# Four tokens' one-hot rows in one broadcast comparison, and gathered rows paced later, in a PEER layer kernel

## The chip, the cores and the metric

The kernel runs on one core of a Trainium2 chip. The metric is the device time of one execution in microseconds, the median of three runs. Engines are named as in the profile: PE is TensorE's matmul, PEld its weight load, DVE is VectorE, ACT is ScalarE, POOL is GpSimd, SP is SyncE. An instruction that only issues a DMA is listed under the engine's queue (SPq, ACTq) or, on POOL, under POOL itself.

## What is computed

One decoder layer on 512 tokens of width 2048: normalisation, two groups of attention heads, an output projection, and then a product-key layer (PEER) whose part of the reference is this, cut to what matters:

```
s_half, i_half = top_k(scores of 2 halves, 16)          # per token and head, 8 heads
top_s, pos = top_k(sums of the two halves' scores, 16)
idx = i * 128 + j                                       # one of 16384 experts
g = softmax(top_s)
u = expert_u[ic];  a = einsum('cd,ced->ce', xc, u)
w = g * gelu(a)
y = einsum('ce,ced->cd', w, expert_v[ic])
```

Each token uses 8 x 16 = 128 experts, and each expert is a row of 2048 floats in `expert_u` and one in `expert_v`.

## The kernel before

About the first 1000 us hold attention, projections and the routing (the top-16 searches). The rest treats the tokens in two ways.

**Tokens 128 to 511, densely.** The "U half" multiplies all 16384 rows of `expert_u` with the 384 tokens, in 128 blocks of 128 rows (`u_block`, loop at L1020). A block is two half-blocks. For each, `u_turn` runs three half-blocks ahead: it issues the block's load in four DMAs (`u_load`, L858, two on SP's queue and two on ACT's), transposes 128x1024 on DVE (L870, `uT`), and `split` makes a high part on ACT (L117) and a low part on DVE (L118). Then come 24 matmuls into `pa` (L883 to L885). At the block's end ACT takes the gelu (L890) and POOL stores `acts_d` (L891). The "V half" (loop from L1050) multiplies the gated activations with the rows of `expert_v`: 16 groups x 4 column quarters x 4 pairs of weights are 256 calls of 18 matmuls (L191 to L193); each weight pair is again split on ACT and DVE, POOL makes the gated `wg` (L1041) ahead of time, and DVE adds the results into `hd` (L1060).

**The gates of these tokens** are spread out during the U half by `dense_gates`. For each of 384 tokens, `expand` makes a one-hot matrix of j on POOL (`oj`, L907), a bf16 one-hot matrix of i on DVE (`on`, L909, four buffers), and from that two gate-weighted versions on ACT (`oi`, L912, two instructions). Seven tokens later `merge` multiplies them on PE (`gps`, L921); ACT and DVE copy and add the result into `stage` (L930, L931), and after each 16 tokens ACT issues the store `gates_d` (L933), 24 stores in all.

**Tokens 0 to 127, by gathering.** `gathered` walks through 256 rows per token: 128 of `expert_u`, then 128 of `expert_v`. For each step POOL issues an indirect DMA (L966) that brings one row for each of 128 tokens (128 x 2048 floats, 1.05 MB) into one of three buffers `gt`, and DVE uses it, L974 in the u part and L977 in the v part. The last step stores `h[0]` (L982).

**What sets the order.** Each engine runs its instructions in an order that the framework fixes when the program is built, by the order in which they are written, by priorities and by a model of when operands are ready. Side work is fed by a `Filler`: each call of `run(budget)` adds to a credit (at most 4.0), and steps are written out while the credit is over zero, each step costing what it yields. A token of `dense_gates` costs 0.17, and each half-block gives it `share` = 36 / (124 - e), with e the first block of the loop. A gathered row costs 2.3; a half-block of the U half gives 1.2, a call of the V half 1.3. `gatherer.drain()` after the last call writes out what is left. The gatherer is `paced`: its instructions are held behind the latest marked DVE instruction.

Of the kernel before, what the change touches and what calls it, by code (L numbers as in the profile page):

```python
# [10 lines left out]
F32 = mybir.dt.float32  # L11
F32R = mybir.dt.float32r
BF16 = mybir.dt.bfloat16
# [3 lines left out]
ALU = mybir.AluOpType  # L17
# [15 lines left out]
PH, NK, TOPK = 8, 128, 16  # L33
SLOTS = PH * TOPK
TG = 128
TD = S - TG
# [16 lines left out]
def block_kernel(ctx, tc, x, positions, norm1_gain, w_in, q_a_gain, w_q_b, kv_a_gain, w_kv_b, mla_q_gain,  # L53
                 mla_k_gain, swa_q_gain, swa_k_gain, swa_sinks, rel_bias_table, group_out_gain, w_out,
                 norm2_gain, peer_w_q, peer_sub_keys, peer_u, peer_v, out):
    nc = tc.nc
# [10 lines left out]
    def pool(name, bufs=1, side=None, stack=ctx, **kw):  # L67
        return stack.enter_context(tc.tile_pool(name=name, bufs=bufs, side=side, reuse_waits="tile", **kw))
# [7 lines left out]
    def acc_tile(name="acc"):  # L76
        return psum.tile([128, 512], F32, name=name, tag="acc", bufs=5)

    def tp_tile(name="tp"):
        return psum.tile([128, 512], F32, name=name, tag="tp", bufs=3)  # L80
# [35 lines left out]
    def split(hi, lo, src):  # L116
        first[0] = nc.scalar.activation(hi, src, AF.Copy)  # L117
        mark[0] = nc.vector.tensor_tensor(lo, src, hi.bitcast(F32), op=ALU.subtract)  # L118
# [551 lines left out]
    for t in range(NT):  # L670
        for i, o in enumerate((o_mla, o_swa)):
# [4 lines left out]
                                           op0=ALU.mult, op1=ALU.mult)  # L676
# [67 lines left out]
    iotb = consts.tile([128, 128], BF16, name="iotb")  # L744
# [59 lines left out]
    def weigh(t, dst):  # L804
        e = exs[t]
        nc.scalar.activation(e, e, AF.Exp)
        z = small.tile([128, PH], F32, name="gz")
        nc.vector.tensor_reduce(z, e, axis=AX.X, op=ALU.add)
        rz = small.tile([128, PH], F32, name="grz")
        nc.vector.reciprocal(rz, z)  # L810
        nc.vector.tensor_tensor(dst.rearrange("p (h s) -> p h s", h=PH), e,
                                rz[:, :, None].to_broadcast([128, PH, TOPK]), op=ALU.mult)
# [49 lines left out]
    def u_turn(n):  # L862
        if n >= 2 * NK:
            return
        e, hf = divmod(n, 2)
        if hf == 0:
            u_load(e + 2)
        hi, lo = part_pair(n, [128, 8, 128])
        uT = up.tile([128, 8, 128], F32, name="uT")
        nc.vector.transpose(uT.rearrange("p k (b j) -> p b k j", j=32),  # L870
                            u_raw[e].rearrange("p b (k i) -> p b k i", k=KC)[:, :, hf * 8:hf * 8 + 8, :])
        split(hi, lo, uT)
        u_parts[n] = hi, lo

    def u_block(e, budget, pace=0.0):
        pa = acc_tile("pa")
        for hf in range(2):
            n = 2 * e + hf
            u_turn(n + 3)
            hi, lo = u_parts.pop(n)  # L880
            for k in range(8):
                kk = hf * 8 + k
                nc.tensor.matmul(pa[:, :TD], hi[:, k, :], xTd[0][:, kk, :], start=kk == 0, stop=False)  # L883
                nc.tensor.matmul(pa[:, :TD], hi[:, k, :], xTd[1][:, kk, :], start=False, stop=False)  # L884
                nc.tensor.matmul(pa[:, :TD], lo[:, k, :], xTd[0][:, kk, :], start=False, stop=kk == KC - 1)  # L885
            filler.run(budget)
            gatherer.run(pace)
        ga = xtp.tile([128, TD], F32, name="ga", bufs=2)
        with tc.issue_after(first[0].ins):
            nc.scalar.activation(ga, pa[:, :TD], AF.Gelu_apprx_tanh)  # L890
        nc.gpsimd.dma_start(acts_d[e], ga)  # L891
# [5 lines left out]
        yield 0.6  # L897

    def dense_gates():
        slT = [gb.tile([128, TD], F32, name=f"slT{r}") for r in range(2)]  # L900
        gT = [gb.tile([128, TD], F32R, name=f"gT{r}") for r in range(2)]
        hot, banks, stages = {}, {}, {}
        LAG = 7

        def expand(t):
            oj = gb.tile([128, NK], F32R, name="oj", bufs=LAG + 2)
            nc.gpsimd.tensor_scalar(oj, iot, slT[1][:, t:t + 1], None, op0=ALU.is_equal)  # L907
            on = gb.tile([128, NK], BF16, name="on", bufs=4)
            nc.vector.tensor_scalar(on, iotb, slT[0][:, t:t + 1], None, op0=ALU.is_equal)  # L909
            oi = gb.tile([128, 2, NK], F32R, name="oi", bufs=LAG + 2)  # L910
            for r in range(2):
                nc.scalar.activation(oi[:, r, :], on, AF.Copy, scale=gT[r][:, t:t + 1].bitcast(F32))  # L912
            hot[t] = oj, oi

        def merge(t):
            oj, oi = hot.pop(t)
            i = t % 2
            if i == 0:
                banks[t // 2] = acc_tile("gps")
            gps = banks[t // 2]  # L920
            nc.tensor.matmul(gps[:, i * 256:(i + 1) * 256], oj, oi.rearrange("p r i -> p (r i)"), start=True, stop=True)  # L921
            if i < 1:
                return
            g0, tb = t // GT, t % GT - 1
            if tb == 0:
                stages[g0] = gb.tile([128, NSG, GT, SG], F32, name="stage", bufs=2)
            stage = stages[g0]
            sums = gps.rearrange("p (t r g e) -> p r t g e", t=2, r=2, e=SG)
            dst = stage[:, :, tb:tb + 2, :].rearrange("p g t e -> p t g e")
            nc.scalar.activation(dst, sums[:, 0], AF.Copy)  # L930
            nc.vector.tensor_tensor(dst, dst, sums[:, 1], op=ALU.add)  # L931
            if tb == GT - 2:
                nc.scalar.dma_start(  # L933
                    bass.AP(tensor=gates_d.tensor, offset=gates_d.offset + g0 * GT * SG,
                            ap=[[TD * SG, 128], [128 * TD * SG, NSG], [1, GT * SG]]),
                    stage.rearrange("p g t e -> p g (t e)"))

        for t in range(1, NT):
            ts = slice((t - 1) * 128, t * 128)
            gt = gb.tile([128, SLOTS], F32, name="gt")  # L940
            weigh(t, gt)
            tp = tp_tile()
            for r in range(2):
                nc.tensor.transpose(tp[:, r * 128:(r + 1) * 128], ijs[t][:, r].rearrange("p h s -> p (h s)"), ident)
            nc.tensor.transpose(tp[:, 256:384], gt, ident)
            for r in range(2):
                nc.scalar.activation(slT[r][:, ts], tp[:, r * 128:(r + 1) * 128], AF.Copy)
            split(gT[0][:, ts], gT[1][:, ts], tp[:, 256:384])
            yield 0.6
        for t in range(TD + LAG):  # L950
            if t < TD:
                expand(t)
            if t >= LAG:
                merge(t - LAG)
            yield 0.17
# [28 lines left out]
    gatherer = Filler(paced=True)  # L984
# [5 lines left out]
    e = 0  # L990
# [11 lines left out]
    gb = pool("gb", stack=stg)  # L1002
    filler.add(dense_gates())
    share = 36.0 / (NK - 4 - e)
    gts, wgs, wb = {}, {}, {}

    def gate_tile(g):
        if g < NSG:
            gg = wp.tile([128, TD, SG], F32, name="gg", bufs=2)
            nc.sync.dma_start(gg, gates_d[g].rearrange("j (t e) -> j t e", e=SG))  # L1010
            gts[g] = gg

    def act_tile(e):
        if e < NK:
            wgs[e] = wp.tile([128, TD], F32, name="wg", bufs=AHEAD)
            nc.sync.dma_start(wgs[e], acts_d[e])
# [1 line left out]
    AHEAD = 5  # L1018
    wp = None
    while e < NK:  # L1020
        u_block(e, share, 1.2)
        e += 1
        if not filler.queue and wp is None:
            stg.close()
            wp = pool("wp", side="right")
            gate_tile(0)
            for i in range(AHEAD):
                act_tile(i)
# [22 lines left out]
    for g in range(NSG):  # L1051
        for c in range(4):
            acc = [acc_tile(), acc_tile(), tp_tile()]
            for i, w in enumerate(weights(v_rows[g * SG * 128:(g + 1) * SG * 128], SG, c * 512, 512, turn=4 * g + c)):
                k0 = 2 * i
                for t in range(NT - 1):
                    products(acc[t], lambda hl, kk, t: wb[g * SG + kk][hl][:, t * 128:(t + 1) * 128], t, k0, SG, w, 512)
                    if k0 == SG - 2:
                        hc = h[t + 1][:, c * 512:(c + 1) * 512]
                        mark[0] = nc.vector.tensor_tensor(hc, acc[t], hc, op=ALU.add)  # L1060
                        if g == NSG - 1:
                            nc.sync.dma_start(out[(t + 1) * 128:(t + 2) * 128, c * 512:(c + 1) * 512], hc)
                nxt = (g + 1) * SG
                if c < 3 and k0 < 4:
                    w_block(nxt + 2 * c + k0 // 2)
                if c == 3 and k0 > 2:
                    w_block(nxt + 4 + k0 // 2)
                gatherer.run(1.3)
    gatherer.drain()


# [23 lines left out]
```

## Time and profile before

| | us |
|---|---|
| median of three runs | 3193.74 |
| runs | 3190.99 to 3194.65 |
| profiled execution, its own time | 3190.16 |
| its span, first to last instruction | 3188.4 |

| engine | busy us | share of the span |
|---|---|---|
| PE | 3074.1 | 96% |
| DVE | 2431.3 | 76% |
| ACT | 1273.9 | 40% |
| POOL | 1275.9 | 40% |

Shares are means over stages with different limits, so the useful views are those by stretch of time: the busy time and the number of instructions of each engine, TensorE's granted clock, and the busy share of the 16 DMA engines. A pipelined matmul counts as busy for longer than it holds the engine, so PE's pace is better read from the count of matmuls in a stretch than from its busy time. The views of waits give for each pair of waiting and releasing instruction the total idle time, the number of waits and the longest; "issue" means that the engine waited for nothing the profile shows.

### The profile page before, as it was taken

What the parts mean: (1) busy time and instruction counts of PE and PEld (TensorE: products, weight loads), DVE (VectorE), ACT (ScalarE), POOL (GpSimd) and SP (SyncE); (2) the same over time, 40 slices, a digit from 0 to 9 for tenths busy, and PEclk for the clock granted to TensorE, in tenths of its full rate; (3) what the DMA queues carried; (4) which work ended last, traced back from release to release, by engine and by line L of the source; (5) the groups of instructions that cost most, each with busy time, mean ns of one, the idle gap of its engine ahead of it and who ended that gap; (6) DMA issues with size and microseconds to landing.
All of it is one profiled execution on the core that took longest, in us unless ns stands there. A gap on an engine that the chain in (4) does not pass through costs nothing.

```text
span 3188.4 us, 42942 instructions
## 1 busy us (share of the span) xinstructions
PE 3074.1 (96%) x15418; PEld 2688.7 (84%) x15418; DVE 2431.3 (76%) x3694; ACT 1273.9 (40%) x2438; POOL 1275.9 (40%) x1260
## 2 busy tenths in 40 slices
PE   8999999989988999899999999999999999999999
PEld 6977768868778999899999998977888888888887
DVE  5425654246999798889989897878888878878874
ACT  5434453232234465555655553332332223322231
POOL 0115320001223476577656654344434433534330
PEclk9998999999989999999999999999999999999999
DMA  5422222243336799999999999989888887878874
GB/s 171 121 80 77 67 96 93 93 129 83 75 94 176 200 285 274 277 268 301 290 286 294 268 281 294 312 320 346 310 318 308 323 312 299 317 286 311 324 265 159
DMA packets 307064, 731.68 MB, mean 229 GB/s; under 512 B 24098, under 2 KB 106274, under 8 KB 269730
## 3 DMA queue, kind: packets, MB, share of 16 engines
q1 hardware_dynamic: 175394, 343.01, 34.3%
q0 software_dynamic: 45056, 293.63, 25.2%
q10 hardware_dynamic: 86400, 92.29, 10.6%
q8 instruction: 122, 2.00, 0.3%
q14 instruction: 92, 0.75, 0.1%
HBM read 666.97 MB, written 61.87 MB: 229 GB/s over the span
## 4 chain that ended last, share of the span: by engine, by line
PE 54%; DVE 15%; DMA 3%; issue 3%; ACT 1%; ACTq 1%; POOL 1%; DVEq 0%; SPq 0%; POOLq 0%
PE acc L191 8%; PE acc L193 7%; PE acc L192 7%; PE pa L885 7%; PE pa L883 7%; PE pa L884 7%; PE tp L191 4%; PE tp L193 3%; PE tp L192 3%; DVE uT L870 3%; DVE wlo L118 3%; DVE gt L974 2%; DMA wg<-acts_d 1%; DVE ulo L118 1%; ACTq L858 1%
## 5 line engine op out<-in xcount | busy, mean ns | idle before, releaser
L885 PE MATMUL pa<-xTd,wlo 128*128 128x384 f32 x1536 | 523.9, 342 | 14.5 <-DVE wlo L118 14.4
L883 PE MATMUL pa<-xTd,whi 128*128 128x384 f32 x1536 | 524.8, 342 | 6.0 <-ACT ga L890 3.5
L884 PE MATMUL pa<-xTd,whi 128*128 128x384 f32 x1536 | 523.6, 341 | 0.0
L907 POOL TENSOR_SCALAR oj<-iot,slT 128x128 fp32r<-128x128 f32 x384 | 416.3, 1092 | 258.2 <-PE gps L921 256.7
L118 DVE TENSOR_TENSOR wlo<-wraw,whi 128x1024 fp32r<-128x1024 f32 (+3 forms) x229 | 285.7, 1254 | 299.3 <-ACT whi L117 292.7
L117 ACT ACTIVATE whi<-wraw 128x1024 fp32r<-128x1024 f32 (+3 forms) x229 | 233.3, 1023 | 515.2 <-PE acc L193 251.1
L966 POOL DMA_INDIRECT gt<-in_peer_v_dram,eidx x128 | 198.7, 1552 | 360.8 <-DVE h L977 329.1
L977 DVE SCALAR_TENSOR_TENSOR h<-gt,w,h 128x2048 f32<-128x2048 f32 x128 | 321.8, 2514 | 13.6 <-DMA gt<-in_peer_v_dram,eidx 13.6
L1041 POOL TENSOR_TENSOR wg<-wg,gg 128x384 f32<-128x384 f32 x128 | 224.1, 1771 | 222.7 <-DMA wg<-acts_d 201.2
L191 PE MATMUL acc<-whi,wh 128*128 128x512 f32 x768 | 307.8, 401 | 2.7 <-ACT wh L117 1.9
L885 PEld LDWEIGHTS pa<-xTd,wlo 128*128 128x128 f32 x1536 | 294.3, 192 | 17.5 <-DVE wlo L118 17.5
L912 ACT ACTIVATE oi<-on,gT 128x128 fp32r<-128x128 bf16 x768 | 253.0, 391 | 138.5 <-issue 76.7
L192 PE MATMUL acc<-wlo,wh 128*128 128x512 f32 x768 | 303.2, 395 | 5.0 <-DVE wlo L118 5.0
L193 PE MATMUL acc<-whi,wl 128*128 128x512 f32 x768 | 304.6, 397 | 0.5 <-DVE wl L118 0.5
L974 DVE CUSTOM_DVE_ANT_0 gt<-gt,xn 128x2048 f32<-128x2048 f32 x128 | 298.7, 2334 | 4.9 <-DMA gt<-in_peer_u_dram,eidx 4.9
L883 PEld LDWEIGHTS pa<-xTd,whi 128*128 128x128 f32 x1536 | 294.7, 192 | 8.0 <-ACT ga L890 3.8
L884 PEld LDWEIGHTS pa<-xTd,whi 128*128 128x128 f32 x1536 | 294.4, 192 | 0.0
L118 DVE TENSOR_TENSOR wlo<-uT,whi 128x1024 fp32r<-128x1024 f32 x192 | 235.7, 1232 | 40.1 <-ACT whi L117 39.8
L117 ACT ACTIVATE whi<-uT 128x1024 fp32r<-128x1024 f32 x192 | 200.9, 1052 | 136.3 <-DVE uT L870 58.8
L192 PE MATMUL acc<-wlo,xT 128*128 128x512 f32 (+2 forms) x624 | 235.6, 378 | 8.8 <-DVE wlo L118 8.7
L191 PE MATMUL acc<-whi,xT 128*128 128x512 f32 (+2 forms) x624 | 237.7, 381 | 4.3 <-ACT xT L117 2.7
L193 PE MATMUL acc<-whi,xT 128*128 128x512 f32 (+2 forms) x624 | 236.2, 379 | 0.0
(301 smaller groups left out, 6742.6 us busy)
## 6 DMA issues: line engine op xcount, KB each, us to landing
wraw<-in_peer_v_dram SPq DMA_DIRECT2D x86, 1024.0 KB
wraw<-in_peer_u_dram ACTq DMA_DIRECT2D x172, 256.0 KB
wraw<-in_peer_u_dram SPq DMA_DIRECT2D x172, 256.0 KB
uraw<-in_peer_v_dram SPq DMA_DIRECT2D x42, 1024.0 KB
acts_d<-ga POOLq DMA_DIRECT2D x128, 192.0 KB
gates_d<-stage ACTq DMA_DIRECT2D x24, 1024.0 KB
gg<-gates_d SPq DMA_DIRECT2D x16, 1536.0 KB
wg<-acts_d SPq DMA_DIRECT2D x128, 192.0 KB
```

The lines of the kernel that those rows point to most:

```text
L117: first[0] = nc.scalar.activation(hi, src, AF.Copy)
L118: mark[0] = nc.vector.tensor_tensor(lo, src, hi.bitcast(F32), op=ALU.subtract)
L191: nc.tensor.matmul(o, lhs(0, kk, t), w[0][:, k, :n], start=kk == 0, stop=False)
L192: nc.tensor.matmul(o, lhs(0, kk, t), w[1][:, k, :n], start=False, stop=False)
L193: nc.tensor.matmul(o, lhs(1, kk, t), w[0][:, k, :n], start=False, stop=kk == kc - 1)
L883: nc.tensor.matmul(pa[:, :TD], hi[:, k, :], xTd[0][:, kk, :], start=kk == 0, stop=False)
L884: nc.tensor.matmul(pa[:, :TD], hi[:, k, :], xTd[1][:, kk, :], start=False, stop=False)
L885: nc.tensor.matmul(pa[:, :TD], lo[:, k, :], xTd[0][:, kk, :], start=False, stop=kk == KC - 1)
L907: nc.gpsimd.tensor_scalar(oj, iot, slT[1][:, t:t + 1], None, op0=ALU.is_equal)
L912: nc.scalar.activation(oi[:, r, :], on, AF.Copy, scale=gT[r][:, t:t + 1].bitcast(F32))
L974: nc.vector.tensor_tensor_reduce(out=gt, in0=gt, in1=xn0, scale=1.0, scalar=0.0, op0=ALU.mult, op1=ALU.add, accum_out=a[:, s:s + 1])
L977: nc.vector.scalar_tensor_tensor(h[0], gt, w[:, s:s + 1], h[0], op0=ALU.mult, op1=ALU.add)
```

## The change

The one-hot matrix `on` is no longer made by one DVE `tensor_scalar` for each token. Every fourth token one DVE `tensor_tensor` compares `iotb`, repeated for four tokens, with four columns of `slT[0]`, each repeated 128 times, and writes four tokens' rows; the tile is then 128x512 and has two buffers instead of four of 128x128. `slT[0]` becomes bf16, as both operands of the comparison are. The gatherer's budget for a half-block of the U half falls from 1.2 to 1.05, and that for a call of the V half rises from 1.3 to 1.4.

```diff
-        slT = [gb.tile([128, TD], F32, name=f"slT{r}") for r in range(2)]
+        slT = [gb.tile([128, TD], BF16 if r == 0 else F32, name=f"slT{r}") for r in range(2)]
...
-        hot, banks, stages = {}, {}, {}
+        hot, banks, stages, ons = {}, {}, {}, {}
...
-            on = gb.tile([128, NK], BF16, name="on", bufs=4)
-            nc.vector.tensor_scalar(on, iotb, slT[0][:, t:t + 1], None, op0=ALU.is_equal)
+            if t % 4 == 0:
+                ons[0] = gb.tile([128, 4, NK], BF16, name="on", bufs=2)
+                nc.vector.tensor_tensor(ons[0], iotb[:, None, :].to_broadcast([128, 4, NK]),
+                                        slT[0][:, t:t + 4, None].to_broadcast([128, 4, NK]), op=ALU.is_equal)
+            on = ons[0][:, t % 4, :]
...
-        u_block(e, share, 1.2)
+        u_block(e, share, 1.05)
...
-                gatherer.run(1.3)
+                gatherer.run(1.4)
```

## Rows read from the trace of the kernel before

**Rows 1.** The page's 40 equal slices of the span, tenths of busy time

```profile
PE   8999999989988999899999999999999999999999
DVE  5425654246999798889989897878888878878874
DMA  5422222243336799999999999989888887878874
```

**Rows 2.** Busy time by stretch: span, then each engine (instructions), clock, DMA share

```profile
1012.40:2096.00 1083.60, 1053.69 (x6094) 1047.07 (x6092) 944.74 (x1284) 572.78 (x1322) 633.24 (x621) 0.99 0.93 280
2096.00:3184.50 1088.50, 1081.30 (x4608) 866.70 (x4608) 881.50 (x722) 326.53 (x382) 429.28 (x259) 1.00 0.81 300
...
2600.00:2700.00 100.00, 100.00 (x430) 80.51 (x429) 79.04 (x65) 29.11 (x32) 35.02 (x22) 1.00 0.85 320
```

**Rows 3.** The same view for shorter stretches of the U half

```profile
1290.00:1310.00 20.00, 11.79 (x51) 10.54 (x50) 12.25 (x17) 10.40 (x26) 5.90 (x7) 0.74 0.96 287
...
1490.00:1530.00 40.00, 35.05 (x188) 34.25 (x187) 34.74 (x48) 19.83 (x46) 26.08 (x24) 0.91 0.98 312
1530.00:1780.00 250.00, 250.00 (x1476) 250.00 (x1475) 233.31 (x337) 146.62 (x350) 165.02 (x169) 1.00 0.97 287
1780.00:1800.00 20.00, 15.63 (x77) 15.40 (x77) 13.74 (x20) 11.65 (x30) 7.48 (x8) 0.83 0.90 265
...
1930.00:1960.00 30.00, 23.32 (x121) 22.80 (x120) 21.99 (x30) 13.95 (x32) 11.30 (x12) 0.89 0.97 299
```

**Rows 4.** Waits in the U half, 1010 to 2096: total us, times, longest

```profile
ACT oi L912 <- issue: 76.7, 10, 13.8
...
DVE on L909 <- ACT oi L912: 41.0, 19, 8.9
...
PE gps L921 <- POOL oj L907: 0.9, 1, 0.9
```

**Rows 5.** ACT in order of time, 1278 to 1304: start, duration, engine, line

```profile
1279.99 0.39 ACTq L933 DMA_DIRECT2D gates_d<-stage  x1
...
1283.10 12.82 ACTq L858 DMA_DIRECT2D wraw<-in_peer_u_dram  x2
```

**Rows 6.** The same view, three later loads, between 1512 and 1952

```profile
1513.66 8.42 ACTq L858 DMA_DIRECT2D uraw<-in_peer_u_dram  x2
...
1773.78 10.46 ACTq L858 DMA_DIRECT2D wraw<-in_peer_u_dram  x2
...
1935.97 9.36 ACTq L858 DMA_DIRECT2D wraw<-in_peer_u_dram  x2
```

**Rows 7.** Groups by line and shape, 1013 to 2096: count, busy, mean ns, idle before

```profile
L974 DVE CUSTOM_DVE_ANT_0 gt<-gt,xn 128x2048 f32<-128x2048 f32 x118 | 270.6, 2293 | 0.0
L966 POOL DMA_INDIRECT gt<-in_peer_u_dram,eidx x119 | 147.2, 1237 | 53.9 <-DVE a L974 27.8 <-issue 12.0 <-DVE on L909 10.5
L909 DVE TENSOR_SCALAR on<-iotb,slT 128x128 bf16<-128x128 bf16 x380 | 92.4, 280 | 41.0 <-ACT oi L912 41.0
L931 DVE TENSOR_TENSOR stage<-stage,gps 128x256 f32<-128x256 f32 x192 | 78.5, 409 | 29.0 <-ACT stage L930 28.9
L890 ACT ACTIVATE ga<-pa 128x384 f32<-128x384 f32 x119 | 56.9, 478 | 55.6 <-PE pa L885 25.8 <-DMA acts_d<-ga 8.2 <-DMA wraw<-in_peer_u_dram 5.3
```

**Rows 8.** Groups by line and shape, whole span

```profile
L977 DVE SCALAR_TENSOR_TENSOR h<-gt,w,h 128x2048 f32<-128x2048 f32 x128 | 321.8, 2514 | 13.6 <-DMA gt<-in_peer_v_dram,eidx 13.6
...
L966 POOL DMA_INDIRECT gt<-in_peer_v_dram,eidx x128 | 198.7, 1552 | 360.8 <-DVE h L977 329.1 <-DMA gt<-in_peer_v_dram,eidx 16.4 <-issue 4.6
...
L118 DVE TENSOR_TENSOR xT<-tp,xT 128x512 fp32r<-128x512 f32 x36 | 23.7, 688 | 7.6 <-ACT xT L117 7.4
...
L781 DVE TENSOR_TENSOR oh<-abf,iot 128x1024 f32<-128x1024 f32 x16 | 19.4, 1213 | 0.1
```

**Rows 9.** The page's DMA queues: packets, MB, share of 16 engines' span

```profile
q0 software_dynamic: 45056, 293.63, 25.2%
```

**Rows 10.** DVE in order of time, 3120 to 3130: the last gathered row

```profile
3124.55 2.35 DVE L977 SCALAR_TENSOR_TENSOR h<-gt,w,h 128x2048 f32<-128x2048 f32 x1
```

## The prediction

> **What bounds the kernel now.** I read the page's slices first. From about the 13th slice on, which is the U half, PE, DVE and the DMA engines are all near nine tenths; in the V half DMA and DVE fall to seven or eight tenths while PE stays full [rows 1]. So I looked at the two halves apart. The U half, 1012.4 to 2096, holds 6094 matmuls in 1083.6 us; the V half holds 4608 in 1088.5 us [rows 2].
>
> The pace is read from the counts. The cleanest long stretch of the U half, 1530 to 1780, has 1476 matmuls in 250 us, 5.90 per us, with PE never idle and the clock granted in full [rows 3]. At that pace 6094 matmuls take 6094 / 5.90 = 1032 us. So the U half loses some 51 us. In the V half, 100 us of full pace hold 430 matmuls, thus 4.19 us for a call of 18 [rows 2]; 4608 / 4.30 = 1072 us, and the remaining 17 us lie mostly in its first 100 us and its end. PE's own work is not touched by the change, so 51 us is the ceiling of what the U half can give.
>
> Where the 51 us lie follows from the same view [rows 3]. A stretch's loss is its length minus its matmuls / 5.90: 11.4 us in 1290 to 1310, 8.1 in 1490 to 1530, 6.9 in 1780 to 1800, 9.5 in 1930 to 1960. These four make 36 us; the other 15 us are spread over the rest. In the four, the granted clock is 0.74 to 0.91, and it is 1.00 in the clean stretch: the lower of its two levels (1.2 and 2.4 GHz) comes with the idle time and is part of the loss.
>
> Their cause is on ACT. At 1279.99 ACT issues the store of gates; at 1283.10 it issues its two loads of the next U block, which hold it for 12.82 us, [rows 5]. Loads hold it again at 1513.66 for 8.42 us, at 1773.78 for 10.46 and at 1935.97 for 9.36 [rows 6]: one long hold inside or just ahead of each of the four bad stretches. ACT does nothing else meanwhile, so no high parts are made, DVE makes no low parts, and PE runs out. In all, ACT's `oi` waited 76.7 us for nothing that the profile shows, ten times, at most 13.8 us [rows 4]. In the four stretches DMA's share is 0.90 to 0.98. Even in the clean stretch it is 0.97, and DVE is busy 233.3 of 250 us, 93% [rows 3]. So at PE's full pace the U half has almost no room on DMA or on DVE: it can't rebuild the lead that covers the next hold.
>
> **The change part by part.** First the pace. The groups by line show 119 gelus after 1013 [rows 7], so the ninth block was just ending, and the gatherer's loop begins there: 120 blocks. Rows written out in the U half: 120 x 2 x 1.2 / 2.3 = 125.2, so 126 with the first; with 1.05 it is 109.6, so 110. Sixteen rows move. (The diff's 0.13 per block is 2 x 0.15 / 2.3.) Each takes with it one DVE instruction of 2.29 us, one POOL issue of 1.24 us [rows 7] and 1.05 MB of DMA. The DMA price: queue 0 used 25.2% of 3188.4 us, 803 us, for 293.6 MB [rows 9], so 1.05 MB cost 2.87 us of all engines. The U half is relieved of 37 us on DVE, 20 on POOL and 46 on DMA. At full pace a block takes 1032 / 119 = 8.67 us; 0.13 x 2.87 = 0.37 us less is 4.3 points: 0.97 becomes 0.93. SP's queue is not touched.
>
> In the V half the same rows cost 16 x 2.51 = 40 us on DVE and 25 us on POOL [rows 8], and 46 us on DMA. DVE goes from 881.5 to 922 of 1088.5 us (85%), POOL from 429 to 454, DMA from 0.81 to 0.85 [rows 2]. What hides it: PE there waits for almost nothing, and its splits run up to four calls ahead (16.8 us) against 2.5 us of one row. I cost it at nothing; if the cover were gone, it would cost at most the 40 us.
>
> Then `on`. Now 384 instructions of 0.28 us, 107 us as a sum of durations and 93 as busy time (92.4 of them in this window) [rows 7]. After: 96 of an unknown length, as no row has this form. The far ends are 0.41 us, what 256 elements take in a two-operand DVE instruction [rows 7], were two done at a time, and 0.69 us for 512 in one by one [rows 8]. I take 0.69, since the nearest row, the comparison L781 with two repeated operands, takes 1.21 us for 1024, one at a time [rows 8]. That makes 66 us, between 39 and 66, and frees 27 to 54 us of DVE. POOL's `oj` may be delayed by a longer two-operand instruction beside it, but PE waits for `oj` 0.9 us in all [rows 4]: nothing.
>
> The Trainium skill speaks against this edit here. Its page "VectorE: DVE Perf Modes" (section "The perf-mode tier table") caps a bf16 `tensor_tensor` at two elements a cycle where a `tensor_scalar` gets four, and ("What auto-detection actually checks") gives two only with steps of one. A repeated column has step zero, so by it the comparison falls to one a cycle, which agrees with L781's row; were only the cap to hold, the sum would be the 39 us.
>
> The buffers: `on` of token t now waits for `oi` of token t - 4; after, a group waits for the group two before, five to eight tokens back. DVE waits there 41.0 us, 19 times, longest 8.9 [rows 4]. Behind it stand transposes and gathered rows that could run while ACT is held. Part of this wait goes; what is late next is the low part, which needs ACT. The longer first wait of a group (0.69 for 0.28 us) delays `oi` by 0.4 us, 96 times; PE's lead covers it, and without the lead it would cost up to 39 us.
>
> The sum for the U half: DVE loses 37 + 27 = 64 us of 945, so 93% in the clean stretch becomes about 87%, and DMA 0.97 becomes 0.93. Holds of 8 to 13 us stay, since the stores of gates stay, but meet a fuller lead of one and a half blocks (13 us) and a shorter backlog. I take half of the 36 us, 18, and 4 of the other 15: 22 us, between 5 and 45. Against the profiled execution: 3190.2 - 22 = 3168. That execution is 3.6 us below the median of 3193.7, so against the median it is 3172; I say 3170.
>
> **The rivals.**
> *The U half loses nothing any more* (0.22). For it: with DMA at 0.97 and the pace at the limit, 4 points may end the backlog altogether. Then 45 of 51 us go: 3147. Against it: a store of 1 MB right before the loads holds ACT by itself.
> *The holds stay as they are* (0.17). The longest begins 3.1 us behind a store of 1 MB [rows 5]; a hold may be the time that the store's own packets take, whatever else is loaded. Then only the 5 us between them go: 3187.
> The Trainium skill ("DMA: Bandwidth & Descriptors", section "Queues, rings and completion order") says that each engine takes turns between the queues that have work. By that rule the hold depends on which queues are busy at that moment, not on the mean load; no row decides it.
> *Slower: more stores fall right ahead of loads* (0.11). The new comparison shifts `expand` against `u_load`. Four of the 24 stores now meet loads so that PE loses some 9 us each. Two more such meetings cost 18 us and outweigh the 5 us of the case before, from one on it is a tie: 3190.2 + 18 - 5 = 3203.
> *Slower: the gather's tail* (0.06). Before, the last row is written at call 130 x 2.3 / 1.3 = 230 of 256, 27 calls or 113 us ahead of 3184.5, thus at 3071; it runs at 3124.55 [rows 10], 53 us late. After, 146 rows end at call 240, 71 us ahead, 3113, and with 53 us of lag at 3166. That leaves 18 us, two and a half rows of 6.9 us, for the store of `h[0]`. From three more rows of lag on, the end moves; five more would give some 3200 even with half the gain in the U half.
> That `on` does not get cheaper (over 1 us each) only takes its 27 us of DVE: it is inside the forecast's range.
>
> **How the numbers follow.** The forecast has 0.44 (3152 to 3186), the others as given. Faster by over 0.2% (6.4 us, about what a measurement of this kernel tells from none) is below 3187.4: 0.44 + 0.22 and 0.04 of the holds' case, 0.70. Within: the rest of that case, 0.13. Slower: 0.17. The range reaches from the full gain, 3147, to 3200: it leaves out what lies beyond either, some 1 in 10 on each side.
>
> **What would show it.** Right: a U half of about 1060 us for its 6094 matmuls, ACT's `issue` waits near 40 us, DMA's share lower there, 96 comparisons of 0.69 us, a V half still at 4.19 us a call, and the last row near 3145. Wrong: loads on ACT held over 8 us as often as before with PE idle behind them, or a gap of PE in the V half before a low part.

## The result, and the profile after

The changed kernel takes 3171.31 us (median; 3159.69 to 3187.33) beside 3191.4 for the kernel before on the same chip; the ratio is 0.995, 95% interval 0.9935 to 0.9964. It is faster by 0.5%, and the forecast of 3170 us with its range holds. A later comparison on another chip (the experiment e12 below) gave 0.9954, 0.9934 to 0.9975. One of e12's ten executions (3362 us) and one of e8's six (4665 us) ran at a lower granted clock, 0.84 and 0.60 on average, and are left out of every median and ratio here. The profiled execution took 3166.97 us, span 3165.3.

The sum came out right, but its terms did not. For every kernel below the **U half** is counted from 1012.4 us to the start of the last gelu (L890), and the **V half** from there to the start of the last L193 matmul. Before, that is 1083.3 and 1088.3 us; after, 1039.6 and 1109.0. So the U half gave back 44 us, twice the 22 of the forecast, and the V half, costed at nothing, lost 21.

The windows of the changed kernel, in the columns of [rows 2]:

```profile
1012.40:2052.00 1039.60, 1036.12 (x6076) 1033.61 (x6074) 902.52 (x969) 570.95 (x1314) 481.87 (x607) 1.00 0.92 277
2052.00:3161.00 1109.00, 1084.40 (x4607) 869.00 (x4608) 902.72 (x749) 325.66 (x383) 464.04 (x273) 0.99 0.83 308
...
2120.00:2140.00 20.00, 15.51 (x56) 12.39 (x57) 19.00 (x21) 3.58 (x5) 5.89 (x4) 0.75 0.71 261
...
2720.00:2740.00 20.00, 13.96 (x51) 11.21 (x52) 16.79 (x15) 3.02 (x4) 3.55 (x3) 0.83 0.88 334
```

In the U half PE is now idle for 3.5 us. At the pace of the clean stretch of [rows 3], 5.90 matmuls per us, its 6076 matmuls take 1030 us, so some 10 us are left of the loss. In the V half the last two rows show where time went: 56 and 51 matmuls in 20 us instead of 86 [rows 2], with the lower clock level granted for part of it.

What held ACT in the U half, from the waits (1010 to 2080, against the `oi` row of [rows 4]) and from ACT in order of time, the longest hold of this profile (against [rows 5, 6]):

```profile
ACT whi L117 <- issue: 43.3, 9, 10.6
...
ACT uhi L117 <- issue: 16.1, 7, 6.2
ACT ga L890 <- issue: 13.9, 7, 5.5
```

```profile
1560.64 0.39 ACTq L936 DMA_DIRECT2D gates_d<-stage  x1
1564.44 5.26 ACTq L858 DMA_DIRECT2D wraw<-in_peer_u_dram  x2
1569.75 1.06 ACT L117 ACTIVATE whi<-uT 128x1024 fp32r<-128x1024 f32 x1 [8.12 <-issue]
```

No load holds ACT longer than 5.26 us, where it was 8.42 to 12.82. In the timeline before, seven of the 24 stores had ACT's next load within 3.2 us; after, two. That count is only a rough sign of the holds: before, one of the four long ones (1935.97) begins 4.27 us behind its store, and three of the seven close pairs hold ACT for less than 3 us.

The comparison itself, and the u rows, by line (the columns of [rows 7]):

```profile
L977 DVE CUSTOM_DVE_ANT_0 gt<-gt,xn 128x2048 f32<-128x2048 f32 x106 | 244.2, 2304 | 4.1 <-DMA gt<-in_peer_u_dram,eidx 4.1
...
L910 DVE TENSOR_TENSOR on<-iotb,slT 128x512 bf16<-128x512 bf16 x94 | 62.5, 677 | 2.9 <-ACT oi L915 2.3
```

It takes 0.677 us, one element at a time like L781 [rows 8]: 512 elements more take L781 0.54 us more. DVE's wait for `oi` in front of it is 2.3 us, where it was 41.0 [rows 4].

The V half's waits, on PE and on DVE. Before (2096 to 3184):

```profile
PE acc L192 <- DVE wlo L118: 5.0, 5, 2.3
```

```profile
DVE h L977 <- DMA gt<-in_peer_v_dram,eidx: 13.6, 8, 2.5
...
DVE gt L974 <- DMA gt<-in_peer_u_dram,eidx: 4.9, 2, 3.4
```

After (from 2050 on):

```profile
PE acc L192 <- DVE wlo L118: 19.3, 6, 7.1
```

```profile
DVE h L980 <- DMA gt<-in_peer_v_dram,eidx: 30.3, 13, 10.3
...
DVE gt L977 <- DMA gt<-in_peer_u_dram,eidx: 20.4, 3, 13.7
```

DVE now waits 51 us for rows that have not landed instead of 18.5, and up to 13.7 us at a time. Low parts stand behind the waiting instruction, and PE waits for them: 19.3 us instead of 5.0, a gap of PE before a low part, which the prediction had named as a sign of being wrong. One such place in order of time, first POOL, then DVE:

```profile
2104.82 7.34 POOL L1044 TENSOR_TENSOR wg<-wg,gg 128x384 f32<-128x384 f32 x5 [13.59 <-DMA wg<-acts_d]
2112.31 0.98 POOL L969 DMA_INDIRECT gt<-in_peer_u_dram,eidx  x1 [0.15 <-issue]
```

```profile
2121.00 2.29 DVE L977 CUSTOM_DVE_ANT_0 gt<-gt,xn 128x2048 f32<-128x2048 f32 x1 [13.73 <-DMA gt<-in_peer_u_dram,eidx]
2123.22 0.08 DVE L977 DVE_READ_ACCUMULATOR2_ANT a<- 128x1 f32 x1
2123.22 2.35 DVE L118 TENSOR_TENSOR wlo<-wraw,whi 128x1024 fp32r<-128x1024 f32 x2
```

POOL waits 13.59 us for a load of activations (`wg`), the fetch of a row stands behind it, and 8.7 us after that fetch DVE's row can start. DVE's own order adds to it here: two rows fetched earlier, at 2084.54 and 2089.55, had landed by 2101.85, but by the semaphores that its instructions wait for, DVE takes them only after this one, at 2131.10 and 2127.28. At 2722 a row waits 10.31 us behind three `wg` products, with the rows in the order of their fetches.

POOL's waits for `wg` are not new. Before (2096 to 3184), then after (2052 to 3161):

```profile
POOL wg L1041 <- DMA wg<-acts_d: 189.0, 44, 13.8
```

```profile
POOL wg L1044 <- DMA wg<-acts_d: 186.6, 41, 13.6
```

So it takes the higher pace of the rows as well for them to reach DVE. That was read from one execution, and made two questions: which part of the change helped the U half and by what, and is POOL's order the cause in the V half?

### The profile page after: what moved, and what is told of

It reads as the page before. It is cut to its first block, busy times and chain, and to the rows that moved or that the text cites. A ratio compares the mean times of both kernels' runs of the same rounds, so it can differ in the third digit from the quotient of the medians.

```text
span 3165.3 us, 42600 instructions
## 1 busy us (share of the span) xinstructions
PE 3059.3 (97%) x15418; PEld 2677.2 (85%) x15418; DVE 2411.7 (76%) x3406; ACT 1272.6 (40%) x2438; POOL 1160.6 (37%) x1260
## 4 chain that ended last, share of the span: by engine, by line
PE 57%; DVE 11%; DMA 5%; issue 3%; POOL 1%; ACT 1%; ACTq 0%; SPq 0%; DVEq 0%; POOLq 0%
PE pa L885 10%; PE pa L883 9%; PE pa L884 9%; PE acc L192 6%; PE acc L191 6%; PE acc L193 6%; PE tp L192 3%; PE tp L191 3%; PE tp L193 3%; DMA wg<-acts_d 2%; DVE wlo L118 2%; DVE h L980 1%; PE gps L924 1%; DMA gt<-in_peer_v_dram,eidx 1%; DVE uT L870 1%
## 5 line engine op out<-in xcount | busy, mean ns | idle before, releaser
L885 PE MATMUL pa<-xTd,wlo 128*128 128x384 f32 x1536 | 514.1, 338 | 13.1 <-DVE wlo L118 13.0
L883 PE MATMUL pa<-xTd,whi 128*128 128x384 f32 x1536 | 518.2, 337 | 1.7 <-ACT whi L117 1.7
L884 PE MATMUL pa<-xTd,whi 128*128 128x384 f32 x1536 | 517.6, 337 | 0.0
L907 POOL TENSOR_SCALAR oj<-iot,slT 128x128 fp32r<-128x128 f32 x384 | 287.2, 757 | 382.1 <-PE gps L924 381.9
L192 PE MATMUL acc<-wlo,wh 128*128 128x512 f32 x768 | 307.5, 400 | 19.3 <-DVE wlo L118 19.3
L1044 POOL TENSOR_TENSOR wg<-wg,gg 128x384 f32<-128x384 f32 x128 | 240.4, 1896 | 226.2 <-DMA wg<-acts_d 199.7
L977 DVE CUSTOM_DVE_ANT_0 gt<-gt,xn 128x2048 f32<-128x2048 f32 x128 | 295.5, 2309 | 20.4 <-DMA gt<-in_peer_u_dram,eidx 20.4
L193 PE MATMUL acc<-whi,wl 128*128 128x512 f32 x768 | 305.5, 398 | 3.7 <-DVE wl L118 3.7
L883 PEld LDWEIGHTS pa<-xTd,whi 128*128 128x128 f32 x1536 | 289.8, 189 | 3.0 <-ACT whi L117 3.0
L884 PEld LDWEIGHTS pa<-xTd,whi 128*128 128x128 f32 x1536 | 289.6, 189 | 0.0
L193 PE MATMUL acc<-whi,xT 128*128 128x512 f32 (+2 forms) x624 | 235.5, 377 | 0.0
```

Of the source, the lines that this page charges most:

```text
L192: nc.tensor.matmul(o, lhs(0, kk, t), w[1][:, k, :n], start=False, stop=False)
L193: nc.tensor.matmul(o, lhs(1, kk, t), w[0][:, k, :n], start=False, stop=kk == kc - 1)
L977: nc.vector.tensor_tensor_reduce(out=gt, in0=gt, in1=xn0, scale=1.0, scalar=0.0, op0=ALU.mult, op1=ALU.add, accum_out=a[:, s:s + 1])
```

## The experiments

The halves are those of the one profiled execution of each kernel. They scatter: the changed kernel's U half was 1039.6 and, in e12, 1046.0, and its whole time lies anywhere from 3160 to 3187. So the medians decide, and a few us between two halves say nothing. "Ratio" is to the kernel before on the same chip.

| kernel | median us | ratio, 95% interval | U half | V half |
|---|---|---|---|---|
| before (first profile) | 3191.40 | | 1083.3 | 1088.3 |
| changed | 3171.31 | 0.9950 (0.9935 to 0.9964) | 1039.6 | 1109.0 |
| e1 comparison alone | 3162.04 | 0.9923 (0.9907 to 0.9938) | 1057.3 | 1087.4 |
| e2 paces alone | 3176.20 | 0.9967 (0.9950 to 0.9984) | 1056.9 | 1101.7 |
| e3 before, stores on SP | 3153.63 | 0.9894 (0.9882 to 0.9907) | 1045.6 | 1088.2 |
| e4 changed, V pace 1.3 | 3169.31 | 0.9945 (0.9933 to 0.9957) | 1043.0 | 1091.8 |
| e5 four single comparisons | 3155.71 | 0.9895 (0.9877 to 0.9914) | 1050.7 | 1087.3 |
| e6 rows: DMA only | 3148.06 | 0.9869 (0.9846 to 0.9891) | 1047.0 | 1085.3 |
| e7 rows: DVE only | 3147.08 | 0.9871 (0.9851 to 0.9892) | 1044.3 | 1079.5 |
| e8 changed, wg on DVE | 3157.41 | 0.9901 (0.9883 to 0.9919) | 1053.2 | 1091.1 |
| e9 e1 and e3 together | 3155.35 | 0.9890 (0.9870 to 0.9909) | 1051.5 | 1085.6 |
| e10 before, eight buffers | 3164.22 | 0.9924 (0.9905 to 0.9943) | 1071.5 | 1086.3 |
| e11 changed, SP and wg on DVE | 3162.37 | 0.9912 (0.9894 to 0.9930) | 1050.6 | 1092.9 |
| e12 changed again | 3175.87 | 0.9954 (0.9934 to 0.9975) | 1046.0 | 1111.6 |

### The two parts apart: e1 and e2

e1 is the changed kernel with the old paces:

```diff
-        u_block(e, share, 1.05)
+        u_block(e, share, 1.2)
...
-                gatherer.run(1.4)
+                gatherer.run(1.3)
```

> The change's comparison alone, with the paces of before (1.2 and 1.3). Theory A (the new comparison shifts the stores of gates away from the loads that follow on ACT's queue, and this, not the relief of the row pace, is most of the U half's gain): U half ends some 30 us earlier than before, V half as before or up to 5 us longer, about 3160 to 3170 us. Theory B (the relief of DMA by 16 rows is what shortens the holds): U half within 10 us of before, about 3180 to 3190 us.

e2 is the kernel before with the new paces alone:

```diff
-        u_block(e, share, 1.2)
+        u_block(e, share, 1.05)
...
-                gatherer.run(1.3)
+                gatherer.run(1.4)
```

> The two paces alone (1.05 and 1.4), with one comparison per token as before. Theory A: the U half gains 10 to 15 us, since stores and loads still meet, and the V half loses some 15 to 20 us as in the changed kernel; in all 3185 to 3200 us. Theory B: the U half gains some 40 us, the V half loses 20, about 3172 us.

The windows of e1, then of e2:

```profile
1012.40:2069.70 1057.30, 1044.85 (x6085) 1040.21 (x6083) 932.54 (x998) 571.76 (x1322) 527.00 (x621) 0.99 0.94 286
2069.70:3157.10 1087.40, 1078.89 (x4608) 865.36 (x4608) 883.01 (x721) 326.53 (x383) 429.62 (x259) 1.00 0.81 301
```

```profile
1012.40:2069.30 1056.90, 1044.58 (x6087) 1041.65 (x6085) 912.79 (x1256) 573.88 (x1321) 583.69 (x607) 0.99 0.91 273
2069.30:3171.00 1101.70, 1082.21 (x4607) 867.27 (x4608) 893.21 (x749) 325.23 (x383) 463.35 (x273) 0.99 0.84 310
```

Each part alone gives some 26 us in the U half, so neither theory held as put: theory A named only the order, theory B only the DMA relief. In e2 eight stores still have their load within 3.2 us, and ACT is held up to 8.00 us, yet PE loses less. The comparison leaves the V half alone (1087.4); the paces cost it 13 us even without the new comparison. The comparison alone (0.9923) did better than the whole change (0.9950, and 0.9954 in e12), though on other chips.

### The cause of the holds: e3

```diff
-                nc.scalar.dma_start(
+                nc.sync.dma_start(
                     bass.AP(tensor=gates_d.tensor, ...
```

> The kernel before, with the 24 stores of gates issued on SP's queue instead of ACT's; nothing else. If ACT's holds behind these stores cost PE its four bad stretches, the holds over 5 us on ACT go and the U half gains 25 to 40 us, V half as before: about 3150 to 3168 us. If PE ran out because DVE and DMA were full and the holds only show it, the gain is under 8 us, 3184 to 3192. SP may be held in place of ACT, and its loads come later: that would give back part.

The windows of e3's two halves:

```profile
1012.40:2058.00 1045.60, 1037.80 (x6085) 1036.71 (x6083) 941.21 (x1284) 574.10 (x1320) 524.95 (x620) 1.00 0.95 290
2058.00:3146.20 1088.20, 1080.50 (x4608) 866.63 (x4608) 881.92 (x721) 326.27 (x383) 433.52 (x259) 1.00 0.81 300
```

One word in the kernel before gives 38 us in the U half and costs nothing in the V half. DVE works as long as before (941 us), and DMA's share is even higher (0.95). No issue of a load on ACT's queue takes over 2.2 us any more. With 3153.6 us (0.9894, against the changed kernel's 0.9950) it is the fastest by its median of the kernels that compute all; e5 and e9 equal it by their ratios.

But the one word moved more than the stores. Count in each trace how many `oi` ACT has begun when it issues a load: in e3 they are 5 more on average than before, up to 16 more, and DVE's wait for `oi`, 41.0 us before [rows 4], is gone. In e1, e5 and e10 they are 8 more, and that wait is 4 to 7 us; in e2 they are as many as before on average, and it is 31 us. So e3 by itself does not tell the other queue from the new order. e7 below keeps the order.

### Why a hold costs PE time: e6 and e7

e6 cuts DVE's work on each gathered row to 64 columns and keeps every fetch:

```diff
-                nc.vector.tensor_tensor_reduce(out=gt, in0=gt, in1=xn0, ...
+                nc.vector.tensor_tensor_reduce(out=gt[:, :64], in0=gt[:, :64], in1=xn0[:, :64], ...
...
-                nc.vector.scalar_tensor_tensor(h[0], gt, w[:, s:s + 1], h[0], ...
+                nc.vector.scalar_tensor_tensor(h[0][:, :64], gt[:, :64], w[:, s:s + 1], h[0][:, :64], ...
```

> The kernel before with the DVE work on the gathered rows cut to 64 of 2048 columns in both halves; every row is still fetched in full (the outputs for the first 128 tokens are not computed). If DVE's 93% is what keeps PE from riding out the holds, the U half falls to 1035 to 1045 us; if the DMA load is, it stays above 1070. V half within 10 us of 1088 either way.

e7 keeps DVE's work and fetches only three rows:

```diff
-            if i < 2 * SLOTS:
-                gt = fetched[i] = gp.tile([128, D], F32, name="gt", bufs=3)
+            if 3 <= i < 2 * SLOTS:
+                fetched[i] = kept[i % 2]
+            elif i < 3:
+                gt = fetched[i] = kept[i] = gp.tile([128, D], F32, name="gt", bufs=3)
...
-                nc.vector.tensor_tensor_reduce(out=gt, in0=gt, ...
+                nc.vector.tensor_tensor_reduce(out=kept[2], in0=gt, ...
```

> The kernel before with only the first three rows fetched; every DVE instruction on rows stays, on the rows already there, and the products of the u part go to the third buffer (the outputs for the first 128 tokens are not computed). If the DMA load makes the holds, ACT's waits of the kind issue fall under 30 us and the U half to 1035 to 1050 us; if DVE is the cause, the U half stays above 1070.

e6, its U half, and ACT at one of its stores:

```profile
1012.40:2059.40 1047.00, 1040.26 (x6082) 1038.37 (x6080) 716.10 (x1283) 573.27 (x1318) 468.75 (x620) 1.00 0.98 290
```

```profile
1780.18 0.39 ACTq L933 DMA_DIRECT2D gates_d<-stage  x1
1781.61 10.09 ACTq L858 DMA_DIRECT2D uraw<-in_peer_u_dram  x2
```

e7's two halves, and ACT at one of its stores:

```profile
1012.40:2056.70 1044.30, 1037.43 (x6076) 1035.71 (x6074) 939.67 (x1282) 573.18 (x1314) 440.94 (x501) 1.00 0.68 172
2056.70:3136.20 1079.50, 1077.64 (x4607) 865.76 (x4608) 868.16 (x721) 328.34 (x383) 261.63 (x124) 1.00 0.50 170
```

```profile
1133.56 0.39 ACTq L933 DMA_DIRECT2D gates_d<-stage  x1
1134.72 1.76 ACTq L858 DMA_DIRECT2D wraw<-in_peer_u_dram  x2
```

Neither kernel computes the outputs of the first 128 tokens. The expectations had asked which of the two it was, DVE or DMA, and it is both. In e6 the DMA engines are fuller than ever (0.98), ACT is held up to 10.09 us, and six of its holds are over 7 us, but with DVE at 68% PE loses next to nothing behind them: the stretch 1780 to 1800 no longer stands out, and the U half is 1047 us. (Its order moved a little, to 2 `oi` fewer ahead of a load on average.) In e7 the order on ACT, DVE and PE is as before, seven stores again have their load within 3.2 us, at the same 1.16 us as before in the place shown, but with the fetches gone and DMA at 0.68 no hold behind one is over 2.82 us, the four bad stretches are gone, and the U half is 1044 us.

Could e7 be faster only because loads land earlier? In the U half of the kernel before, none of the waits of PE and DVE ends with a load. All but 0.8 us of DVE's end with ACT, the largest of them this:

```profile
DVE wlo L118 <- ACT whi L117: 41.7, 33, 5.8
```

So holds on ACT cost PE its time. The store need not be right ahead, though. Single issues of over 2.5 us begin 0.6 to 8.9 us behind a store on ACT's queue, like this one of e10, 6.4 us behind its store:

```profile
1915.26 8.73 ACTq L858 DMA_DIRECT2D uraw<-in_peer_u_dram  x1
```

With the stores on SP's queue (e3, e9, e11) there are none. So in these runs a long hold came with a store on the same queue a few us before and full DMA engines, and it cost PE time where DVE was too busy to have built a lead.

### What the comparison did: e5 and e10

e5 makes the new tile with four old comparisons:

```diff
             if t % 4 == 0:
                 ons[0] = gb.tile([128, 4, NK], BF16, name="on", bufs=2)
-                nc.vector.tensor_tensor(ons[0], iotb[:, None, :]..., slT[0][:, t:t + 4, None]..., op=ALU.is_equal)
+                for i in range(4):
+                    nc.vector.tensor_scalar(ons[0][:, i, :], iotb, slT[0][:, t + i:t + i + 1], None, op0=ALU.is_equal)
```

> The kernel before with the new tile and its grouping (four tokens' rows at every fourth token, two buffers) but made by four single comparisons, as many DVE instructions as before. Theory A (what the comparison brought is the order: stores of gates and loads meet less often): U half near that of the comparison alone, 1057 us, in all 3160 to 3168. Theory B (it is the DVE time freed): U half as before, 1083, in all 3182 to 3192.

e10 changes one number of the kernel before:

```diff
-            on = gb.tile([128, NK], BF16, name="on", bufs=4)
+            on = gb.tile([128, NK], BF16, name="on", bufs=8)
```

> The kernel before with eight buffers for a token's one-hot rows instead of four, so that DVE can run eight tokens ahead of ACT as in the changed kernel; comparisons stay one by one and where they were. If the longer reach is what the grouping brought, the U half falls to 1050 to 1060 us, in all 3155 to 3165. If it is the place of the work in the order (stores against loads), the U half stays at 1075 to 1085, in all 3180 to 3192.

The U halves of e5 and e10:

```profile
1012.40:2063.10 1050.70, 1043.18 (x6088) 1039.57 (x6086) 937.77 (x1281) 572.97 (x1321) 549.97 (x620) 1.00 0.94 288
```

```profile
1012.40:2083.90 1071.50, 1052.04 (x6100) 1046.78 (x6098) 939.94 (x1291) 574.39 (x1324) 567.46 (x622) 0.99 0.93 283
```

e5 has as many DVE instructions as before and gains as much as the new comparison, or a little more (3155.7). So the broadcast instruction is not needed for the gain. But e5 does not keep all of the old cost: its four comparisons stand back to back and take 0.70 to 0.74 us together, and all of them 69.2 us of busy time, where the old ones took 92.4 and the new ones take 62.5. What speaks against the saved DVE time as the cause is e3, where DVE is busy 941 us of the U half instead of 945 and the U half still gains 38 us; but it is not shown. What e1 and e5 share besides is the tile of four tokens with two buffers, and the order that the framework then fixes, with `oi` further ahead of the loads and one store of 24 that has its load within 3.2 us. Eight single buffers also give 24 us (3164.2), with the comparisons one by one; but this, too, changed the fixed order (one store within 3.2 us), so a longer reach of DVE ahead of ACT and the place of the stores are not told apart. That stays open. e10's profiled execution took 3176 us, the longest of its six, so its U half is at the upper end.

### The V half: e4, e8, e11 and e12

e4 gives the changed kernel's V half the old pace:

```diff
-                gatherer.run(1.4)
+                gatherer.run(1.3)
```

> The changed kernel with the V half's pace back at 1.3, so that 16 rows are moved but not made up. Tail theory: the last row is written out only at the end of the last call, runs some 50 us later, and the execution ends some 40 to 50 us after the last matmul: about 3200 to 3215 us. The V half's stalls behind late rows get fewer (PE's V half 5 to 15 us shorter) since rows come as slowly as before. Rival: DVE catches up with the rows at the end, and the tail costs under 10 us: 3160 to 3172.

The window of e4's V half, and then DVE in order of time at its end, the last three rows:

```profile
2055.40:3147.20 1091.80, 1080.60 (x4608) 866.60 (x4608) 896.48 (x744) 324.46 (x383) 456.78 (x272) 1.00 0.84 309
```

```profile
3151.01 2.34 DVE L980 SCALAR_TENSOR_TENSOR h<-gt,w,h 128x2048 f32<-128x2048 f32 x1
3155.59 2.35 DVE L980 SCALAR_TENSOR_TENSOR h<-gt,w,h 128x2048 f32<-128x2048 f32 x1 [2.23 <-DMA gt<-in_peer_v_dram,eidx]
3159.24 2.35 DVE L980 SCALAR_TENSOR_TENSOR h<-gt,w,h 128x2048 f32<-128x2048 f32 x1 [1.29 <-DMA gt<-in_peer_v_dram,eidx]
```

PE's V half is 17 us shorter, though 148 rows run in it instead of 152, so the higher pace of the rows, and not the mere number, made it long. POOL waits for `wg` as before, 222.6 us in all. The tail exists: the execution ends 19.6 us after the last L193 matmul's start instead of 4.3. But it costs 15 us, not 40 to 50: with its other work running out, DVE takes rows every 3.7 to 4.6 us. The two effects cancel within the uncertainty.

e8 moves the product `wg` from POOL to DVE in the changed kernel:

```diff
-        nc.gpsimd.tensor_tensor(wg, wg, gts[g][:, :, i], op=ALU.mult)
+        nc.vector.tensor_tensor(wg, wg, gts[g][:, :, i], op=ALU.mult)
```

> The changed kernel with the product wg moved from POOL to DVE, 128 instructions of some 0.5 us, so that POOL issues a row's fetch without standing behind a wait for a load of activations. If that wait is what makes rows late in the V half, DVE's waits for rows fall from 51 us to under 20 and the V half returns to 1088 to 1095 us, in all about 3145 to 3160. Rival (the DMA engines or the tighter pace make rows late): V half stays over 1102 us. A second rival: DVE itself then waits for those loads with low parts behind it, and the V half gets longer, over 1110.

The window of e8's V half, and then DVE's waits in it:

```profile
2065.60:3156.70 1091.10, 1078.96 (x4607) 866.84 (x4608) 918.46 (x872) 327.71 (x383) 296.24 (x150) 1.00 0.84 313
```

```profile
DVE wg L1044 <- DMA wg<-acts_d: 26.4, 9, 6.5
...
DVE gt L977 <- DMA gt<-in_peer_u_dram,eidx: 12.8, 2, 7.1
...
DVE h L980 <- DMA gt<-in_peer_v_dram,eidx: 7.6, 10, 0.9
```

The V half is back at 1091 us, at the full row pace and with DVE busier than in the changed kernel (918 us instead of 903). DVE's waits for rows fall from 51 to 20 us. The new wait for activations, 26 us, is on DVE now but at most 6.5 us long, and the lead covers it. So POOL's order, a fetch behind a product that waits for its load or runs long, is the cause of most of the V half's loss, at this pace: either the slower pace (e4) or the other engine (e8) takes 17 to 18 of the 21 us away. The edit has a price at the end of the U half, where the first `wg` are made: DVE waits 13.33 us for their loads there, with low parts behind it, and PE waits 9.3 us for one.

e11 puts e3's and e8's edits on the changed kernel:

> The changed kernel with the stores of gates on SP's queue and the product wg on DVE. If the two causes are the right ones, the U half is 1035 to 1042 us and the V half 1088 to 1092, in all 3140 to 3148: faster than the changed kernel by 24 to 30 us. If the V half's loss comes from rows as such, it stays over 1100 and the whole at 3155 or more.

e12 runs the changed kernel once more:

> The changed kernel as it is, beside the others on one chip. If the row pace takes back part of what the comparison gives, it is slower than the comparison alone by 6 to 12 us, at 3166 to 3175; its V half is 12 to 21 us longer than before's, and how long differs from execution to execution. If the longer V half of its first profile was one execution's mishap, it is at 3150 to 3160.

The windows of e11:

```profile
1012.40:2063.00 1050.60, 1040.41 (x6096) 1038.81 (x6094) 908.97 (x977) 570.02 (x1323) 416.97 (x604) 1.00 0.90 275
2063.00:3155.90 1092.90, 1080.48 (x4607) 867.80 (x4608) 918.09 (x872) 327.81 (x383) 295.86 (x150) 0.99 0.84 313
...
1950.00:1970.00 20.00, 14.76 (x69) 13.80 (x70) 17.02 (x17) 4.77 (x6) 3.10 (x4) 0.74 0.91 282
```

The second of two loads on ACT, and DVE just after:

```profile
1951.66 0.32 ACTq L858 DMA_DIRECT2D wraw<-in_peer_u_dram  x1
```

```profile
1952.08 3.94 DVE L1044 TENSOR_TENSOR wg<-wg,gg 128x384 f32<-128x384 f32 x5 [14.28 <-DMA wg<-acts_d]
```

The V half of e12:

```profile
2058.40:3170.00 1111.60, 1086.74 (x4608) 869.39 (x4608) 901.10 (x749) 324.94 (x383) 461.66 (x273) 0.99 0.83 307
```

e12 repeats the long V half (1111.6), so it was no mishap. e11's V half is as expected, its U half is not: 1050.6 - 6096 / 5.90 = 17 us lost, most of them between 1930 and 1970, where the first loads for the V half begin. DVE waits 14.28 us there for `wg`, as in e8. And ACT stands for 11.5 us between the two loads of a U block. That is no long issue, as each takes 0.32 us: the second begins at 1951.66, just after the landing of a load that SP could issue only when the last store of gates on its queue had landed. The same gap stands in e3 and e9. Nor does e11 beat e3: the comparison, the moved rows and `wg` on DVE together brought nothing once the stores were on SP's queue.

### Do the two cures add? e9

e9 is e1 with e3's edit.

> The new comparison with the paces of before, and the stores of gates on SP's queue. If the holds on ACT are the whole of the loss that both edits treat, the two gains don't add: U half 1035 to 1046 us, V half 1088, in all 3143 to 3155, at most 10 us under the stores on SP alone (3153.6). If they are two causes, 26 and 38 us add up to the floor of 1032 and the time falls to 3138 to 3143.

The window of e9's U half:

```profile
1012.40:2063.90 1051.50, 1040.36 (x6083) 1038.52 (x6081) 930.24 (x998) 568.38 (x1318) 483.62 (x621) 0.99 0.94 288
```

3155.35 us beside 3153.63 for e3 on another chip, with ratios of 0.9890 and 0.9894: they don't add. The comparison and the other queue cure the same loss. Which of their common effects does it, shorter holds or `oi` further ahead, is not told apart here.

## Why the prediction was right, and where it was not

- **What bounds the kernel now**: right. ACT held by loads behind a store, on full DMA engines and with DVE too full to rebuild the lead, was the reading of [rows 3, 5, 6]. e7 shows the holds and the DMA engines' part at an unchanged order, e6 the part of DVE, and e3, whose order moved too, agrees on the store. The ceiling of 51 us for the U half held: no kernel's U half was under 1032 us.
- **The size of the U half's gain**: the step "I take half of the 36 us" was too small. Measured: 44 us, the rival to which 0.22 was given (37 in e12). Both parts of the change helped, and the forecast did not foresee how far the fixed order itself would move: holds of 8 to 13 us, which it let stay, are 5.26 us at most.
- **The new comparison's price**: 0.69 us taken, 0.677 measured, and 30 us of DVE freed where 27 were taken. The Trainium skill's page "VectorE: DVE Perf Modes" (section "What auto-detection actually checks") led to one element a cycle for a repeated column, and the trace agrees: 512 elements in 0.677 us, 1024 in 1.213. **Its use** was not as put: four old comparisons back to back gain as much (e5), so the new instruction as such is not what brought the gain.
- **The rows' use**: sixteen were to move; by the end of the U half 104 have run instead of 118, so fourteen did. That the relief of DVE and DMA helps agrees with e2 (26 us, with holds of up to 8.00 us), but e2's order differs in places too.
- **The V half**: the step that failed is "I cost it at nothing; if the cover were gone, it would cost at most the 40 us". The cover of four calls was set against 2.5 us of DVE work for a row, but what a row costs there is a wait for its DMA, up to 13.7 us, with low parts behind it on DVE and with POOL's wait for `wg` ahead of its fetch. The trace before had both: L977 waited 13.6 us in all for its rows [rows 8], and POOL 189.0 us for `wg`, at most 13.8 us at a time. The measured price is 13 to 23 us (e2, changed, e12).
- **ACT's `issue` waits**: forecast near 40 us, measured 73 (43.3, 16.1 and 13.9). Before, the other targets had some 37 us beside the 76.7 of `oi`, which the forecast left out. The total hardly says what PE loses: e2's is 110 us and e1's 78 at the same U half. The longest hold does, where DVE is about as busy as before. With the loss taken as U half minus matmuls / 5.90: 12.82 us and a loss of 50 before, 8.73 and 38 in e10, 8.00 and 25 in e2, 7.33 and 26 in e1, 6.44 and 19 in e5, 5.26 and 10 in the changed kernel. In e6, with DVE at 68%, it is 10.09 and 16.
- **The holds' rival**, that a store's own packets make the hold: e7 speaks against it, as the same pair 1.16 us apart holds ACT 1.76 us once the row fetches are gone. The Trainium skill's page "DMA: Bandwidth & Descriptors" (section "Queues, rings and completion order") has each DMA engine take turns between queues with work; that a hold shrinks when one queue's work is taken away agrees, but no run here shows the turns.
- **The tail's rival**: the last row of the changed kernel runs at 3131.88 us, 13 us ahead of the 3145 named, and the end stays with PE. Its price past the end was overstated (e4).

The number was right by luck: two errors of some 21 us each, in the U half and in the V half, cancelled.

## What to carry to other kernels

Where an engine both computes and issues DMAs, look for its waits of the kind "issue" and for what was issued just before; moving one large store to a queue that computes nothing (e3) was worth more here than the whole change. A step moved to a stage with slack must be priced by its waits and by what stands ahead of it on each in-order queue, POOL's included, and not by its busy time. And when an edit speeds up a kernel, try a variant that keeps its order but not its saving, and check in the trace that it does both: e5 was meant so and kept most of the saving, and one word (e3) moved the order of whole engines. The clean experiment here was the one whose order stayed (e7).

## What was not expected of the hardware

- A load of 0.25 MB pieces on ACT's queue, usually issued in 0.86 us for two, held the engine for up to 12.82 us when a store of 1 MB had been issued 3.1 us ahead and the DMA engines were full; with the rows' fetches gone, 2.82 us for the same pair. It is no wait for the load's buffer: each of the seven longest issues of the kernel before begins 0.03 us after the DVE transpose that frees it.
- POOL's `oj` took 287 us in all instead of 416, a mean of 757 ns instead of 1092, with the same instruction; the shortest is 590 ns in both. It is not the form of the comparison: e3 keeps the old one and has a mean of 704 ns, e7, with the order of before, 993. What lengthens it stays open.
